# A masked softmax on one core: engines programmed by hand in one critical section, and a mask that skips the left half of the columns behind a branch

## The chip, the cores and the metric

The kernel runs on one core of a Trainium2 chip. The metric is the device time of one execution in microseconds (us). A core has several engines that run their own instruction streams side by side: DVE (the vector engine), ACT (the scalar engine, here for the exponential), POOL, PE (not used for work here) and SP, which in this kernel only issues transfers. Transfers between the large memory (DRAM) and the on-chip memory are done by 16 DMA engines; a transfer of a whole batch is cut over all 16, and each of them works its queue off in order. A semaphore is a counter by which one engine, or a finished transfer, tells another that it may go on.

## The reference

The input `x` has 16 batches, 8 heads and 256 x 256 float32 values for each; each batch has one length. Softmax is taken along the last axis over the first `length` columns, and all columns from there on are zero.

```python
batch, heads, seq_q, seq_k = 16, 8, 256, 256
lengths = np.random.randint(seq_k // 2, seq_k, size=batch)
...
for b in range(batch):
    length = lengths[b]
    masked = x[b, :, :, :length].copy()
    masked = masked - np.max(masked, axis=-1, keepdims=True)
    exp_masked = np.exp(masked)
    result[b, :, :, :length] = exp_masked / np.sum(exp_masked, axis=-1, keepdims=True)
```

The lengths are thus at least 128. The 16 that are drawn, the same in every run, lie between 157 and 252. `x` and the result have 33.55 MB each, and a batch 2 MB each way.

## The kernel before, in words

The 2048 rows of a batch (8 heads x 256) are laid on 128 partitions with 16 rows of 256 columns each, so that one tile `x_tile` holds a whole batch, 128 x 4096 values. There are 12 such buffers (`slots`). All work is done in place in the buffer.

A framework schedules the kernel: it takes the operations in the order of the program text, puts them on their engines, may change the order on an engine by its own estimate, and adds the semaphore waits.

- Line 42, ACT's queue: the 16 lengths are copied to every partition (`len_bcast`, a transfer of 16 KB).
- Line 48, SP: the loads of the batches. The first 12 are issued ahead; load `b + 10` is issued after the store of batch `b`, for `b` from 2 on, into the buffer whose store was issued two batches earlier, and waits for that store. The framework gives the transfers eight semaphores in turn, so that a transfer waits until the one eight places before it has landed.
- Lines 55, 57, 61: POOL writes the column numbers, DVE adds one half and turns the lengths to float.
- Line 67, DVE, once a batch: `cap`, one row of 256 values on every partition, is (column + 0.5 - length) x -1e30. It is a very large positive number in the columns to keep and a very large negative one in the others.
- Line 80, DVE, twice a batch (8 rows per partition each): the minimum of `x_tile` and `cap`, called a clip below. Kept columns stay as they are, and the others become very negative, so that their exponential is zero.
- Line 87, ACT, 16 times a batch: the exponential of one row per partition, with the row's sum as a second result. The maximum is not subtracted.
- Line 93, DVE, twice a batch: the reciprocals of 8 sums. Line 95, DVE, 16 times a batch: each row times its reciprocal.
- Line 102, SP: the store of the batch.

On DVE the scheduler runs about one half batch ahead: a clip of the next half stands between the reciprocals and the multiplications of the last one. SP's queue is in the order of the text: loads 0 to 11, stores 0 to 2, then load 12, store 3, load 13, store 4, load 14, store 5, load 15 and stores 6 to 15.

Of the kernel before, what the change touches and what calls it, by code (L numbers as in the profile page):

```python
# [1 line left out]

# [4 lines left out]


F32 = mybir.dt.float32  # L10
ALU = mybir.AluOpType
EXP = mybir.ActivationFunctionType.Exp


@with_exitstack
def kernel(
    ctx: ExitStack,
    tc: tile.TileContext,
    x: bass.AP,
    lengths: bass.AP,  # L20
    out: bass.AP,
):
    nc = tc.nc
    P = nc.NUM_PARTITIONS

    batch, heads, seq_q, seq_k = x.shape
    rows = heads * seq_q
    assert rows % P == 0
    nt = rows // P

    x_f = x.rearrange("b h q k -> b (h q) k").rearrange("b (p t) k -> b p t k", p=P)
    out_f = out.rearrange("b h q k -> b (h q) k").rearrange("b (p t) k -> b p t k", p=P)

    slots = 12
    ahead = slots - 2

    singles = ctx.enter_context(tc.tile_pool(name="singles", bufs=1))
    work = ctx.enter_context(tc.tile_pool(name="work", bufs=slots))
    small = ctx.enter_context(tc.tile_pool(name="small", bufs=4))

    len_bcast = singles.tile([P, batch], mybir.dt.int64)
    nc.scalar.dma_start(out=len_bcast, in_=lengths.partition_broadcast(P))

    tiles = {}

    def load(b):
        tiles[b] = work.tile([P, nt, seq_k], F32, name="x_tile", tag="x_tile")
        nc.sync.dma_start(out=tiles[b], in_=x_f[b])

    for b in range(min(slots, batch)):  # L50
        load(b)


    iota_i32 = singles.tile([P, seq_k], mybir.dt.int32)
    nc.gpsimd.iota(iota_i32, pattern=[[1, seq_k]], base=0, channel_multiplier=0)  # L55
    iota_h = singles.tile([P, seq_k], F32)
    nc.vector.tensor_scalar(  # L57
        out=iota_h, in0=iota_i32, scalar1=0.5, scalar2=None, op0=ALU.add
    )
    len_f32 = singles.tile([P, batch], F32)  # L60
    nc.vector.tensor_copy(out=len_f32, in_=len_bcast.bitcast(mybir.dt.int32)[:, ::2])  # L61

    for b in range(batch):
        t = tiles.pop(b)

        cap = small.tile([P, seq_k], F32, name="cap", tag="cap")
        nc.vector.tensor_scalar(  # L67
            out=cap,
            in0=iota_h,
            scalar1=len_f32[:, b : b + 1],  # L70
            scalar2=-1.0e30,
            op0=ALU.subtract,
            op1=ALU.mult,
        )
        row_sum = small.tile([P, nt], F32, name="row_sum", tag="row_sum")
        inv_sum = small.tile([P, nt], F32, name="inv_sum", tag="inv_sum")
        half = nt // 2
        for h in range(2):
            s = slice(h * half, (h + 1) * half)
            nc.vector.tensor_tensor(  # L80
                out=t[:, s, :],
                in0=t[:, s, :],
                in1=cap[:, None, :].to_broadcast([P, half, seq_k]),
                op=ALU.min,
            )
            for j in range(h * half, (h + 1) * half):
                nc.scalar.activation(  # L87
                    out=t[:, j, :],
                    in_=t[:, j, :],
                    func=EXP,  # L90
                    accum_out=row_sum[:, j : j + 1],
                )
            nc.vector.reciprocal(out=inv_sum[:, s], in_=row_sum[:, s])  # L93
            for j in range(h * half, (h + 1) * half):
                nc.vector.tensor_scalar(  # L95
                    out=t[:, j, :],
                    in0=t[:, j, :],
                    scalar1=inv_sum[:, j : j + 1],
                    scalar2=None,
                    op0=ALU.mult,  # L100
                )
        nc.sync.dma_start(out=out_f[b], in_=t)
        n = b + ahead
        if b >= 2 and slots <= n < batch:
            load(n)


# [1 line left out]
_INS = ['x', 'lengths']  # L109
_OUTS = [((16, 8, 256, 256), 'float32')]  # L110


# [23 lines left out]
```

## Time and profile before

| | |
|---|---|
| Time, median of 9 runs | 166.24 us (166.08 to 166.58) |
| The profiled execution: its own time | 166.05 us |
| Its span in the profile | 164.3 us |
| DRAM read and written | 33.57 MB and 33.55 MB, 409 GB/s over the span |
| First load and lengths transfer issued | 0.74 and 0.73 us after the start |
| First instruction of DVE on data | 9.83 us, after the lengths have landed |
| Last store issued | 156.0 us |
| From issue to landing, stores | 7.4 us at least, 27.8 in the median, 39.7 at most |
| DVE's instructions | 338 busy ones; 341 in the program |

How to read the profile: the first lines give each engine's busy time, its share of the span and the number of its instructions. Then the span is shown in 40 equal slices of 4.1 us, a digit for each (9 is 90% busy or more); the line DMA is the mean busy share of the 16 DMA engines. The lines on queues give packets, megabytes and the share of the 16 engines' span; q1 is SP's queue, q10 is ACT's, and q14 brings the engines' instructions. The chain that ended last is followed back from the last instruction. A group line has the source line, the engine, the operation, what is written and read with its shape and the number of instructions, then the busy time and the mean of one in nanoseconds, then the idle time just before them. A line of windows gives, for a stretch of time, each engine's busy microseconds and instructions, the clock of PE, the mean share of the DMA engines (packets are counted where they start, so a short window can be over 1) and what they moved. Beside these views the trace has the start and length of each packet and the time of each of the 16 marks by which the DMA engines report their part of a transfer as done.

### The profile page before, as it was taken

To read this page: it belongs to the slowest core of one execution; us is meant where nothing else is said; L and a number is where in the kernel's file an instruction comes from. 1 tells how busy PE (TensorE), PEld (TensorE's weight loads), DVE (VectorE), ACT (ScalarE), POOL (GpSimd) and SP (SyncE) were. 2 spreads that over 40 slices of the span, in tenths; PEclk is the share of its full clock that TensorE was granted. 3 is DMA by queue.
4 is the path that set the end of the run, shared out by engine and by line. 5 is a ranking of instruction groups with operands and counts; after the bars stand their busy time and mean duration, and the time that the engine had idled before them with its cause. 6 is when DMAs were issued, how large, how long until landed. Compare 5 with 4: busy or idle time off the path is not lost.

```text
span 164.3 us, 981 instructions
## 1 busy us (share of the span) xinstructions
DVE 145.0 (88%) x338; ACT 105.9 (64%) x513; POOL 0.5 (0%) x5
## 2 busy tenths in 40 slices
DVE  0059999999999999999999999999999999999700
ACT  0038999177977376938887676937695886947300
POOL 1000000000000000000000000000000000000000
DMA  6999999999999999999999999999999999999793
GB/s 164 334 412 423 443 425 427 421 435 435 423 427 435 423 421 435 435 427 427 423 431 421 431 433 411 439 431 427 427 427 439 431 425 431 433 435 423 339 391 144
DMA packets 4759, 67.18 MB, mean 409 GB/s; under 512 B 656, under 2 KB 656, under 8 KB 656
## 3 DMA queue, kind: packets, MB, share of 16 engines
q1 hardware_dynamic: 4608, 67.11, 96.9%
q14 instruction: 7, 0.06, 0.1%
q10 hardware_dynamic: 144, 0.02, 0.1%
HBM read 33.57 MB, written 33.55 MB: 409 GB/s over the span
## 4 chain that ended last, share of the span: by engine, by line
DVE 86%; DMA 6%; ACT 2%; issue 1%; DVEq 0%; ACTq 0%
DVE x_tile L80 42%; DVE x_tile L95 39%; DMA len_bcast<-in_lengths_dram 6%; DVE inv_sum L93 2%; ACT x_tile L87 2%; DVE cap L67 2%; DVEq L131 0%; DVE iota_h L57 0%; DVE len_f L61 0%; ACTq L131 0%
## 5 line engine op out<-in xcount | busy, mean ns | idle before, releaser
L87 ACT ACTIVATE x_tile<-x_tile 128x256 f32<-128x256 f32 x256 | 102.5, 402 | 37.9 <-issue 23.3
L80 DVE TENSOR_TENSOR x_tile<-x_tile,cap 128x2048 f32<-128x2048 f32 x32 | 72.3, 2261 | 0.0
L95 DVE TENSOR_SCALAR x_tile<-x_tile,inv_sum 128x256 f32<-128x256 f32 x256 | 69.9, 347 | 0.1
L87 ACT ACTIVATION_READ_ACCUMULATOR x_tile<-x_tile 128x1 f32 x256 | 47.9, 187 | 0.0
L61 DVE CAST len_f<-len_bcast 128x16 f32<-128x16 int32 x1 | 0.2, 175 | 9.8 <-DMA len_bcast<-in_lengths_dram 9.8
L87 ACT ACT_TABLE_LOAD x1 | 1.3, 1283 | 9.7 <-DMA x_tile<-in_x_dram 9.7
L93 DVE RECIPROCAL inv_sum<-row_sum 128x8 f32<-128x8 f32 x32 | 6.1, 194 | 1.0 <-ACT x_tile L87 1.0
L67 DVE TENSOR_SCALAR cap<-iota_h,len_f 128x256 f32<-128x256 f32 x16 | 4.8, 316 | 0.0
L55 POOL IOTA iota_i<- 128x256 int32 x1 | 0.3, 342 | 0.4 <-PEq L131 0.4
L57 DVE TENSOR_SCALAR iota_h<-iota_i 128x256 f32<-128x256 int32 x1 | 0.3, 286 | 0.0
L120 POOL MEMSET const-bfloat16-1.0<- 128x1 bf16 x1 | 0.1, 102 | 0.0
L120 POOL MEMSET const-uint8-127<- 128x1 uint8 x1 | 0.1, 102 | 0.0
L120 POOL MEMSET const-float32-0.0<- 128x1 f32 x1 | 0.1, 99 | 0.2 <-issue 0.2
L120 POOL MEMSET const-float32-1.0<- 128x1 f32 x1 | 0.1, 99 | 0.0
## 6 DMA issues: line engine op xcount, KB each, us to landing
x_tile<-in_x_dram SPq DMA_DIRECT2D x16, 2048.0 KB, 25.8
out_dram<-x_tile SPq DMA_DIRECT2D x16, 2048.0 KB, 27.8
len_bcast<-in_lengths_dram ACTq DMA_DIRECT2D x1, 16.0 KB, 9.1
```

The costliest lines, as they stand in the source:

```text
L55: nc.gpsimd.iota(iota_i32, pattern=[[1, seq_k]], base=0, channel_multiplier=0)
L57: nc.vector.tensor_scalar(out=iota_h, in0=iota_i32, scalar1=0.5, scalar2=None, op0=ALU.add)
L61: nc.vector.tensor_copy(out=len_f32, in_=len_bcast.bitcast(mybir.dt.int32)[:, ::2])
L67: nc.vector.tensor_scalar(out=cap, in0=iota_h, scalar1=len_f32[:, b : b + 1], scalar2=-1.0e30, op0=ALU.subtract, op1=ALU.mult,)
L80: nc.vector.tensor_tensor(out=t[:, s, :], in0=t[:, s, :], in1=cap[:, None, :].to_broadcast([P, half, seq_k]), op=ALU.min,)
L87: nc.scalar.activation(out=t[:, j, :], in_=t[:, j, :], func=EXP, accum_out=row_sum[:, j : j + 1],)
L93: nc.vector.reciprocal(out=inv_sum[:, s], in_=row_sum[:, s])
L95: nc.vector.tensor_scalar(out=t[:, j, :], in0=t[:, j, :], scalar1=inv_sum[:, j : j + 1], scalar2=None, op0=ALU.mult,)
L120: nc = _bacc.Bacc("TRN2", target_bir_lowering=False, num_devices=1)
```

## The change

All operations stand in one critical section, in which the framework neither orders nor adds waits: each engine's stream and every semaphore are written out by hand. Entering and leaving the section puts a few control instructions (a no-op, waits, branches) on the engines. Every load and every store has a semaphore of its own (`s_ld`, `s_st`).

- SP issues the same transfers in the same order; the first 12 loads go without any wait, a store waits for `s_out`, loads 12 to 15 wait for the store of the buffer's earlier batch, and at the end SP waits for all stores.
- DVE reads the 16 lengths into registers (two load instructions for 32 words, line 65 of the kernel after).
- The mask of batch `b + 1` is put ahead of the reciprocals and multiplications of batch `b`. It is one clip of the right half of the columns for all 16 rows, 128x16x128, and one of the left half behind a branch that is taken past it when the length is 128 or more (lines 124 and 136 of the kernel after).
- DVE waits for its own reciprocal by a semaphore (`s_v`) before it multiplies. ACT waits once a batch (`s_min`) and reports each half batch (`s_exp`).
- `row_sum` and `inv_sum` have their own place for every batch, and `cap` has four in turn as before.

DVE's program has 377 instructions in place of 341. The core of the diff, with the removed lines left out:

```diff
+    with tc.tile_critical(no_gpsimd_drain=True):
...
+        nc.sync.dma_start(out=xt[0], in_=x_f[0]).then_inc(s_ld[0], 16)
+        nc.scalar.dma_start(out=len_i, in_=lengths.partition_broadcast(P)).then_inc(s_len, 16)
+
+        _, words = nc.values_load_multi_w_load_instructions(
+            lengths.bitcast(I32)[None, :],
+            engines=[DVE],
...
+        lens = words[::2]
...
+        for b in range(1, slots):
+            load(b)
+        for b in range(batch):
+            nc.sync.wait_ge(s_out, b + 1)
+            nc.sync.dma_start(out=out_f[b], in_=xt[b % slots]).then_inc(s_st[b], 16)
+            n = b + slots - behind
+            if b >= behind and n >= slots and n < batch:
+                nc.sync.wait_ge(s_st[n - slots], 16)
+                load(n)
+        for b in range(batch):
+            nc.sync.wait_ge(s_st[b], 16)
...
+        def clip(b, lo, hi):
+            t = xt[b % slots]
+            return nc.vector.tensor_tensor(
+                out=t[:, :, lo:hi],
+                in0=t[:, :, lo:hi],
+                in1=cap[:, b % 4, None, lo:hi].to_broadcast([P, nt, hi - lo]),
                 op=ALU.min,
             )
...
+        def mask(b):
+            if b + 1 < batch and b + 1 not in cap_at:
+                cap_at[b + 1] = make_cap(b + 1)
+            nc.vector.wait_ge(s_v, cap_at[b])
+            nc.vector.wait_ge(s_ld[b], 16)
+            with nc.vector.If(lens[b] < mid):
+                clip(b, 0, mid)
+            clip(b, mid, seq_k).then_inc(s_min, 1)
...
+        mask(0)
+        for b in range(batch):
+            if b + 1 < batch:
+                mask(b + 1)
+            t = xt[b % slots]
+            for h in range(2):
+                s = slice(h * half, (h + 1) * half)
+                nc.vector.wait_ge(s_exp, 2 * b + h + 1)
+                step(nc.vector.reciprocal(out=inv_sum[:, b, s], in_=row_sum[:, b, s]))
+                nc.vector.wait_ge(s_v, v)
+                for j in range(h * half, (h + 1) * half):
+                    ins = nc.vector.tensor_scalar(
...
+            ins.then_inc(s_out, 1)
...
+        for b in range(batch):
+            t = xt[b % slots]
+            nc.scalar.wait_ge(s_min, b + 1)
+            for j in range(nt):
+                ins = nc.scalar.activation(
...
+                if (j + 1) % half == 0:
+                    ins.then_inc(s_exp, 1)
```

## The prediction

> **What bounds the kernel now.** I read the busy lines and the slices of the page first, then the DMA queues, the chain of work that ended last, the groups, and at last the windows of the final microseconds. The page at first accuses DVE:
>
> ```profile
> DVE 145.0 (88%) x338; ACT 105.9 (64%) x513; POOL 0.5 (0%) x5
> ...
> DMA  6999999999999999999999999999999999999793
> ...
> q1 hardware_dynamic: 4608, 67.11, 96.9%
> q14 instruction: 7, 0.06, 0.1%
> ...
> DVE 86%; DMA 6%; ACT 2%; issue 1%; DVEq 0%; ACTq 0%
> ```
>
> The chain gives DVE 86% of the span. But a chain names one path, and the slices show a second resource just as full: the 16 DMA engines stand at 9 tenths from the second slice to the 38th, and SP's queue (q1) holds them for 96.9% of the span. Both resources run from the first microseconds to the last, so which of them sets the end has to be read at the end itself:
>
> ```profile
> core 0: us, DVE busy (x) ACT busy (x) POOL busy (x), PEclk, DMA share, GB/s
> ...
> 10.00:58.00 48.00, 47.96 (x110) 35.57 (x172) 0.00 (x0) 1.00 1.01 429
> 58.00:114.00 56.00, 56.00 (x127) 40.50 (x199) 0.00 (x0) 1.00 1.01 427
> 114.00:153.00 39.00, 38.46 (x94) 29.02 (x143) 0.00 (x0) 1.00 1.01 431
> 153.00:155.00 2.00, 1.45 (x6) 0.48 (x3) 0.00 (x0) 1.00 0.94 401
> 155.00:156.00 1.00, 0.95 (x4) 0.00 (x0) 0.00 (x0) 1.00 0.31 131
> 156.00:157.00 1.00, 0.00 (x0) 0.00 (x0) 0.00 (x0) 1.00 0.69 295
> 157.00:158.00 1.00, 0.00 (x0) 0.00 (x0) 0.00 (x0) 1.00 0.65 279
> 158.00:159.00 1.00, 0.00 (x0) 0.00 (x0) 0.00 (x0) 1.00 1.21 508
> ```
>
> The last two columns are to be read. From 10 to 153 us the DMA engines have no gap (share 1.01) at 427 to 431 GB/s, in loads, mixture and stores alike. The only dip is at 155 to 158 us, when most engines have drained and the last store is issued at 156.0. It is worth 0.69 + 0.31 + 0.35 = 1.35 us of all 16 engines, and it is the only thing in this trace that a faster DVE can fill. I then asked whether it sets the end. The trace keeps 16 completion marks for each transfer, one per DMA engine. For the last but one store they lie at 155.27 to 157.26 us on 14 engines and at 158.21 and 158.56 on the two latest. For the last store 14 lie at 162.06 to 162.24 and two at 163.01 and 163.33. The two late engines took 163.01 - 158.21 = 4.80 and 163.33 - 158.56 = 4.77 us for it, no more than the 4.9 us that every transfer takes on an engine throughout (latest marks of the first four loads: 9.64, 14.51, 19.42, 24.32). So **the two engines that end the kernel never waited for DVE**; the dip is on the other 14. The kernel is bound by the latest DMA engine, and DVE runs just beside it.
>
> **What the change removes.** The drawn lengths are 157 to 252, all at or above 128, so every branch skips the left half. 32 clips of 128x2048 become 16 of 128x16x128, as many elements each:
>
> ```profile
> L80 DVE TENSOR_TENSOR x_tile<-x_tile,cap 128x2048 f32<-128x2048 f32 x32 | 72.3, 2261 | 0.0
> L95 DVE TENSOR_SCALAR x_tile<-x_tile,inv_sum 128x256 f32<-128x256 f32 x256 | 69.9, 347 | 0.1
> L93 DVE RECIPROCAL inv_sum<-row_sum 128x8 f32<-128x8 f32 x32 | 6.1, 194 | 1.0 <-ACT x_tile L87 1.0
> ```
>
> 72.3 / 2 = 36.1 us leave DVE: 145.0 - 36.1 = 108.9 us, with some 0.24 us twice a batch now exposed between reciprocal and first multiplication (150.07 to 150.30 us in the timeline), 16 x 0.48 = 8 us: 117 us, 7.3 a batch against 9.0 (93.92 - 75.92 = 18.0 for two). ACT needs 6.4 a batch (16 x 0.40 from start to start), so DVE stays the slower of the two and is 9.8 + 117 = 127 us in, if nothing stops it. What is late next is the transfer queue, which was never early: 32 x 4.9 = 157 us on each engine. Its order stays as it is, twelve loads, three stores, then load and store in turn, then stores. The last load lands at 114.0 us now, so batch 15 is ready at about 125 and the last store is issued some 30 us sooner. Of the 36 us I therefore book **zero**: the 14 engines close their dip and end earlier, the two late ones do not.
>
> **What it adds on DVE.** All of this has cover. The first store takes its turn behind twelve loads, at 64.1 us (latest mark of load 11), and batch 0 would be ready near 20; the last store has the 30 us above. The 16 compare-and-branch pairs and the two register loads of the lengths are not in this trace. Nearest rows: a DVE semaphore instruction of 21 ns below; above, for the register loads, the 9.1 us landing of the small lengths transfer, each, 18 us at most, which moves batch 0 from 20 to 38, still under 64; for a branch, a whole 8 KB instruction load waited out, 0.31 us in the trace's packets behind one 16 KB packet of 0.61: 2 x 0.92 = 1.8 a batch, with which DVE takes 9.1, its pace of now. None reaches the path by waiting alone. If the cover went, one microsecond a batch would cost 16. DVE also waits for load b+1 before it multiplies batch b; behind that wait stand the reciprocals and multiplications of b, and SP's store of b waits for them. The worst case is batch 14 behind load 15 at 114.0, when its store's turn comes after 150.4 (first mark of store 13): covered by 30 us.
>
> On SP, loads 7 to 11 no longer wait for a free one of eight semaphores, but seven loads were already queued, so nothing starts sooner. SP waits for store b-2 before it loads into that slot, with store b+1 queued behind that wait, exactly as now (43.6 us over four such waits), and two stores are in the rings meanwhile. The lengths transfer leaves from ACT's queue beside the first load as now, so the slow first 9 us (304 GB/s) stay.
>
> **What lies on the path.** Two ends remain. At the start the critical section puts a no-op, a wait of SP on its own semaphore and a branch ahead of the first load; SP's control instructions at the close follow each other at 0.06 us, so 3 x 0.06 = 0.18 us, between 0.06 and 0.4 (the 0.4 being the barrier hop of the first 0.65 us). At the close SP goes through two branches, a no-op that collects five semaphores and another branch, and the other engines wait for it: seven steps of 0.06 less the three trailing waits that go, 0.24 us, between 0 and 0.6. Third, instruction loads share the DMA engines: seven of 8 KB during the run, 0.31 us each in the trace's packets, after which the latest mark of that moment is some 0.45 us later (29.22 to 34.56 is 5.34 us where 4.9 is usual). DVE's program grows from 341 to 377 instructions before its separate waits, so between none and one more such load, on one engine, which need not be the last: 0 to 0.45, I take 0.13.
>
> Sum: 166.05 (profiled execution) + 0.18 + 0.24 + 0.13 = 166.60. That execution lies 0.19 under the median of nine, 166.24, so against the median the sum is 166.79. I forecast **166.7**, between the two.
>
> [...]
>
> **Rivals.**
> 1. *The late engines are late by accident* (faster). Their lag of some 3.3 us was collected in steps from 0.8 us, beside instruction loads and at the turns from loads to stores. If another pace of DVE and ACT spreads these over other engines, the third latest sets the end: 157.26 + 4.85 = 162.1 instead of 163.3, with the two ends 166.24 - 1.2 + 0.4 = 165.4. With all engines even (mean mark 156.07 + 4.85 = 160.9) it would be 164.2. For it: the dip of 1.35 us is real. Against it: the nine runs lie within 0.5 us, so the lag repeats. Chance 0.21, all faster.
> 2. *A jump reloads code* (slower). If each taken branch fetches 8 KB, 16 packets of 0.31 us, 0.45 each with what they push aside, land on the one engine that serves DVE: + 7.2 us, and 166.24 + 0.4 + 7.2 = 173.8. It decides from about one reload a batch. Against it: seven reloads in the whole run now, as many as straight code needs. Chance 0.07.
> 3. *The ends cost more* (slower): both upper bounds and a whole extra load, 0.4 + 0.6 + 0.45 = 1.45, 167.7. Chance 0.10.
> 4. *The skip does not act*, and DVE runs both halves, 32 clips and 145 us. The transfers still bound: 166.7. Chance 0.02.
>
> My forecast, the ends at 166.4 to 167.1, holds the remaining 0.60.
>
> **Chances and range.** A measurement of this kernel can tell some 0.2%, 0.33 us, from no change, so "same" is 165.91 to 166.57. The forecast (with rival 4, 0.62) splits into 0.40 slower, 0.19 same, 0.03 faster; rivals 2 and 3 add 0.17 slower, rival 1 adds 0.21 faster: faster 0.24, same 0.19, slower 0.57. The range reaches into rivals 1 and 3: 165.3 to 168.0.
>
> **What would show it.** Right: DVE near 109 us busy, x16 clips of 2.2 to 2.3 us; DVE idle in the last 30 us; the last stores waiting long in the rings (landing after 30 us or more, where 7.4 is the shortest now); no dip before the last microseconds; the same late end of one or two engines. The q14 row shows the reloads: 7 or 8 bears out the sum, over 20 is rival 2. First load issued at 0.9 instead of 0.74 us shows the start. Wrong: a last mark well before 163 us after the start (rival 1), or DMA share below 0.95 between 10 and 150 us.

## The result, and the profile after

The kernel after takes 167.07 us in the median of 10 runs (166.76 to 167.36); the kernel before, with 30 runs by then, 166.25. The ratio is 1.0048, 95% interval 1.0036 to 1.0060: the change makes the kernel some half per cent slower. The forecast was 166.7, slower. The profiled execution of after is one of its shorter ones, 166.33 us with a span of 164.6, against 166.05 and 164.3 before, so a profile alone shows 0.28 of the 0.82 us.

The page of the kernel after, the same lines as were shown of before:

```profile
DVE 113.9 (69%) x322; ACT 104.9 (64%) x513; POOL 0.5 (0%) x5
...
DMA  2999999999999999999999999999999999999981
...
q1 hardware_dynamic: 4608, 67.11, 96.0%
q14 instruction: 7, 0.06, 0.1%
...
DVE 64%; DVEq 11%; ACT 4%; issue 2%; SPq 0%
```

DVE gave up 145.0 - 113.9 = 31.1 us, and the DMA line is as full as it was. The chain still begins with DVE, at 64%, in a kernel that got slower while DVE got faster: a share of the chain is no price. The groups, in the same order of columns as before:

```profile
L152 DVE TENSOR_SCALAR x<-x,inv_sum 128x256 f32<-128x256 f32 x256 | 70.2, 349 | 1.1
...
L124 DVE TENSOR_TENSOR x<-x,cap 128x2048 f32<-128x2048 f32 x16 | 36.6, 2287 | 0.0
L102 DVE CAST len_f<-len_i 128x16 f32<-128x16 int32 x1 | 0.2, 175 | 17.9 <-issue 17.9
L149 DVE RECIPROCAL inv_sum<-row_sum 128x8 f32<-128x8 f32 x32 | 6.3, 198 | 1.7 <-ACT x L166 1.7
```

16 clips of 2.29 us are left: the skip acts. DVE now starts at 17.9 us. The windows (engines, clock of PE, DMA share, GB/s):

```profile
1.00:10.00 9.00, 0.00 (x0) 1.28 (x1) 0.34 (x1) 1.00 0.74 284
10.00:58.00 48.00, 38.07 (x103) 36.04 (x179) 0.00 (x0) 1.00 1.01 430
58.00:114.00 56.00, 55.44 (x157) 50.83 (x252) 0.00 (x0) 1.00 1.01 429
114.00:153.00 39.00, 20.37 (x65) 16.73 (x84) 0.00 (x0) 1.00 1.01 431
...
157.00:158.00 1.00, 0.00 (x0) 0.00 (x0) 0.00 (x0) 1.00 1.07 459
158.00:159.00 1.00, 0.00 (x0) 0.00 (x0) 0.00 (x0) 1.00 0.99 426
159.00:160.00 1.00, 0.00 (x0) 0.00 (x0) 0.00 (x0) 1.00 0.73 311
160.00:161.00 1.00, 0.00 (x0) 0.00 (x0) 0.00 (x0) 1.00 0.31 131
161.00:162.00 1.00, 0.00 (x0) 0.00 (x0) 0.00 (x0) 1.00 0.27 115
162.00:163.00 1.00, 0.00 (x0) 0.00 (x0) 0.00 (x0) 1.00 0.04 16
```

The dip at 155 to 158 us is gone, the rate between 10 and 153 us is the same, and the end is a slope: from 159 us on fewer and fewer DMA engines have anything left. The completion marks of the last store say it by engine: 12 of them at 160.07 to 161.23 us, the last four at 162.26, 162.77, 162.93 and 163.24. Before, the last mark was at 163.33.

The stores now wait in the queue and not for DVE: the last one is issued at 134.6 us and lands 28.6 us later, and none lands sooner than 19.0 us after its issue, where 7.4 was the least before.

```profile
L80 SPq DMA_DIRECT2D out_dram<-x x16: 332/338/695, 30.2 to 134.6; - x16
...
DMA to landing us min/median/max: 19.0/33.5/39.8
```

### The profile page after: what moved, and what is told of

It is laid out like the page before. It is cut to its first block, busy times and chain, and to the rows that moved or that the text cites. A ratio compares the mean times of both kernels' runs of the same rounds, so it can differ in the third digit from the quotient of the medians.

```text
span 164.6 us, 968 instructions
## 1 busy us (share of the span) xinstructions
DVE 113.9 (69%) x322; ACT 104.9 (64%) x513; POOL 0.5 (0%) x5
## 4 chain that ended last, share of the span: by engine, by line
DVE 64%; DVEq 11%; ACT 4%; issue 2%; SPq 0%
DVE x L152 39%; DVE x L124 20%; DVEq L65 10%; ACT x L166 4%; DVE inv_sum L149 2%; DVE cap L109 2%; DVEq L136 0%; DVE iota_h L104 0%; DVE len_f L102 0%; DVEq L199 0%; SPq L50 0%
## 5 line engine op out<-in xcount | busy, mean ns | idle before, releaser
L166 ACT ACTIVATE x<-x 128x256 f32<-128x256 f32 x256 | 102.3, 402 | 25.5 <-DVE x L124 25.5
L152 DVE TENSOR_SCALAR x<-x,inv_sum 128x256 f32<-128x256 f32 x256 | 70.2, 349 | 1.1
L166 ACT ACTIVATION_READ_ACCUMULATOR x<-x 128x1 f32 x256 | 48.0, 187 | 0.0
L124 DVE TENSOR_TENSOR x<-x,cap 128x2048 f32<-128x2048 f32 x16 | 36.6, 2287 | 0.0
L102 DVE CAST len_f<-len_i 128x16 f32<-128x16 int32 x1 | 0.2, 175 | 17.9 <-issue 17.9
L109 DVE TENSOR_SCALAR cap<-iota_h,len_f 128x256 f32<-128x256 f32 x16 | 5.5, 349 | 0.0
```

What stands on the lines that cost most here:

```text
L102: step(nc.vector.tensor_copy(out=len_f, in_=len32[:, ::2]))
L109: nc.vector.tensor_scalar(out=cap[:, b % 4, :], in0=iota_h, scalar1=len_f[:, b : b + 1], scalar2=-1.0e30, op0=ALU.subtract, op1=ALU.mult,)
L124: return nc.vector.tensor_tensor(out=t[:, :, lo:hi], in0=t[:, :, lo:hi], in1=cap[:, b % 4, None, lo:hi].to_broadcast([P, nt, hi - lo]), op ...
L152: ins = nc.vector.tensor_scalar(out=t[:, j, :], in0=t[:, j, :], scalar1=inv_sum[:, b, j : j + 1], scalar2=None, op0=ALU.mult,)
L166: ins = nc.scalar.activation(out=t[:, j, :], in_=t[:, j, :], func=EXP, accum_out=row_sum[:, b, j : j + 1],)
```

## The experiments

All times are medians; every ratio is to the kernel before, run beside it on the same chip.

**One part alone: the right half in the framework (run tile_right).**

```diff
 nc.vector.tensor_tensor(
-    out=t[:, s, :],
-    in0=t[:, s, :],
-    in1=cap[:, None, :].to_broadcast([P, half, seq_k]),
+    out=t[:, s, seq_k // 2 :],
+    in0=t[:, s, seq_k // 2 :],
+    in1=cap[:, None, seq_k // 2 :].to_broadcast([P, half, seq_k // 2]),
     op=ALU.min,
 )
```

> The kernel before with one part of the change alone: its two clips a batch take only the right 128 columns (the left half is left out without any branch; with these lengths it changes nothing). DVE loses some 36 us of work. Theory (the latest DMA engine ends the kernel and never waits for DVE): no gain, 166.25 us, between 165.9 and 166.6; the dip in the DMA share at 155 to 158 us goes. Rival 1 (the dip counts, the freed DVE time shortens the end): 164.9 us. Rival 2 (DVE is the bound, as the chain of waits says): about 135 to 140 us of DVE work and then the transfers, again 164 to 165 us, with the last store issued long before.

Measured: 166.36 us, ratio 0.9997 (0.9988 to 1.0007). DVE is busy for 112.7 us, the last store is issued at 136.6 in place of 156.0, and nothing is gained. The last marks (14 engines at 160.0 to 161.1, two at 163.58 and 163.75) show why: the 14 end earlier, the two do not. Both rivals fall.

**The section without register loads and branch (run crit_right).**

```diff
-        _, words = nc.values_load_multi_w_load_instructions(...)
...
-            with nc.vector.If(lens[b] < mid):
-                clip(b, 0, mid)
             clip(b, mid, seq_k).then_inc(s_min, 1)
```

> The kernel after without the register loads and without the branch: the right half is clipped, the left half is left out. DVE starts at some 9 us in place of 17.9. Theory (register loads and branches are covered, the loss lies in the two ends of the critical section): as the kernel after, 167.0 us, between 166.7 and 167.4. Rival (the branch, or the 15 us register load, costs the time): 166.3 us or less.

Measured: 166.89 us, ratio 1.0037 (1.0024 to 1.0050), which overlaps that of the kernel after. So registers and branches cost 0.2 us, if anything. The same half mask in the framework, on the same chip, took 166.36 us: the section with its hand-written streams costs 0.53 us even without registers and branches. The 0.2 us are little for what the register loads do to DVE in the kernel after (rows of its sequencer: number, ns at least, in the median and at most, first and last start):

```profile
L65 DVEq TENSOR_LOAD <-in_lengths_dram_ptr x1: 1783/1783/1783, 1.0 to 1.0; - x1
L65 DVEq TENSOR_LOAD <-in_lengths_dram x1: 15041/15041/15041, 2.8 to 2.8; - x1
```

The two loads hold DVE for 16.8 us; a delay of 8 us at DVE's start goes under, as the first store's turn comes at 64 us. A branch takes 56 ns, and there are as many instruction loads, seven, as before.

**The section with the whole mask: where the cover ends (run crit_full).**

```diff
-            with nc.vector.If(lens[b] < mid):
-                clip(b, 0, mid)
-            clip(b, mid, seq_k).then_inc(s_min, 1)
+            clip(b, 0, seq_k).then_inc(s_min, 1)
```

(The register loads go too.)

> The kernel after with the mask of before: one clip of all 256 columns a batch, no register load, no branch. Each batch costs DVE 2.2 us more, so 7.2 + 2.2 = 9.4 us a batch, 9.5 + 16 x 9.4 = 160 us, and the last store is issued at 160 and lands at 167.5. Theory (DVE is covered only as long as it issues the last store before its turn at some 155 to 158 us): 170.5 us, between 169 and 172. Rival (DVE work does not matter in this section at all): 167.0 us.

Measured: 168.62 us, ratio 1.0130 (1.0112 to 1.0147). The sign is the theory's, the size is 1.9 us under it and just below its range: a batch takes DVE 9.28 us, not 9.4, the last store is issued at 159.0, not 160, and its last mark comes 6.5 us later, not 7.5: at 165.49, 4.9 us after that of the store before it. The windows show the hole that a late DVE makes in the transfers, which no run with the half mask has:

```profile
142.00:146.00 4.00, 3.96 (x14) 4.00 (x21) 0.00 (x0) 1.00 0.88 377
146.00:150.00 4.00, 3.96 (x3) 1.48 (x8) 0.00 (x0) 1.00 1.06 449
150.00:154.00 4.00, 3.96 (x17) 4.00 (x22) 0.00 (x0) 1.00 0.25 107
154.00:158.00 4.00, 3.93 (x17) 2.13 (x12) 0.00 (x0) 1.00 0.78 328
158.00:162.00 4.00, 0.95 (x4) 0.00 (x0) 0.00 (x0) 1.00 1.03 434
```

So the half mask is worth 168.62 - 166.89 = 1.7 us inside the section, where a batch of the whole mask takes DVE 9.28 us in place of 9.0, and nothing in the framework.

**The transfers alone, in the framework (run tile_copy) and in the section (run crit_copy).** Every operation on DVE, ACT and POOL is taken out; loads and stores keep their order, and a store waits for its load.

> The transfers of the kernel before alone: the same loads and stores in the same order, with the lengths transfer, and no work on DVE, ACT or POOL (the output is x itself; all of the softmax is left out). Theory (the latest DMA engine sets the end): the time stays within 1.5 us of the kernel before, 165.0 to 166.3 us, best value 165.5; what is missing are the instruction loads of DVE and ACT, which the late engines collect. Rival (work on DVE or ACT sets the end): 163 us or less.

Measured: 164.03 us (163.23 to 164.71), ratio 0.9864 (0.9836 to 0.9892). This is 1.0 us below the theory's range and 1.0 above the rival's, and decides for neither as worded. All but 2.3 of the 166.34 us of the kernel before are those of the bare transfers, and what makes the 2.3 was still to be shown.

> The transfers of the kernel after alone, in the critical section, with no work on the other engines (the output is x itself; all of the softmax is left out), no register load and no branch. Theory (the loss lies in entering and leaving the section): slower than the transfers in the framework by the same 0.6 to 0.8 us as the kernel after against the kernel before. Rival (the loss comes from the programs on DVE and ACT): the same as the transfers in the framework, within 0.2 us.

Measured: 166.34 us, ratio 0.9977 (0.9954 to 1.0000), 2.3 us over the transfers in the framework, with a wide spread (164.63 to 166.57). The section is dearer without any program on DVE or ACT, which goes against the rival; but 2.3 is three times the theory's 0.6 to 0.8. Of the profiled pair 0.5 us lie at the close (1.21 us from the last mark to the end, against 0.72) and 1.45 at the last mark (162.84 against 161.39). With no instruction load at all, the latest engine of the section's transfers ends 2.40 us behind the first (160.44); its latest mark makes steps of 5.16, 5.52 and 5.47 us at the transfers that end at 78.7, 103.8 and 114.2, while loads and stores alternate. In the framework, too, three steps there are longer than the usual 4.9: 5.20, 5.20 and 5.15.

**Programs beside the transfers (run copy_instr).** To the transfers alone, 256 exponentials and 339 multiplications on scratch rows are added, which nothing waits for:

```diff
...
+    for i in range(256):
+        nc.scalar.activation(out=scr_a, in_=scr, func=EXP, accum_out=sums[:, i : i + 1])
...
+    for i in range(339):
+        nc.vector.tensor_scalar(out=scr_v, in0=scr, scalar1=0.5, scalar2=None, op0=ALU.mult)
```

> The transfers alone, as in the run tile_copy, and beside them DVE and ACT work through programs as long as those of the kernel before (339 multiplications and 256 exponentials) on scratch rows that no transfer touches (all of the softmax is left out). Theory (8 KB instruction loads share the DMA engines, and the engines that serve them end late): some 7 instruction loads in the run in place of none, and the time back from 164.0 to 165.5 to 166.4 us, best value 166.0. Rival (it is the work on the batch buffers themselves that slows the transfers): 164.0 us as without programs.

Measured: 165.79 us, ratio 0.9967 (0.9956 to 0.9978): 1.76 of the 2.3 us between the bare transfers and the kernel before come back with programs that touch no batch buffer. First the queues of the bare transfers, then those with programs:

```profile
q1 hardware_dynamic: 4608, 67.11, 97.9%
q10 hardware_dynamic: 144, 0.02, 0.1%
HBM read 33.57 MB, written 33.55 MB: 414 GB/s over the span
```

```profile
q1 hardware_dynamic: 4608, 67.11, 96.8%
q14 instruction: 7, 0.06, 0.1%
q10 hardware_dynamic: 144, 0.02, 0.1%
HBM read 33.57 MB, written 33.55 MB: 409 GB/s over the span
```

The row q14 is the one that is new. It is 0.1% of the DMA engines' time, yet the last engine lies 1.6 us behind the first at the end of the bare transfers (161.39 and 159.84) and 3.5 behind with programs (163.27 and 159.80). The run adds the instruction loads and the work on the scratch rows together; no run has one without the other.

**Fewer instructions on DVE (run tile_mul1).** The clip of tile_right, and a half batch multiplied at once:

```diff
...
-            for j in range(h * half, (h + 1) * half):
-                nc.vector.tensor_scalar(
...
+            nc.vector.tensor_tensor(
+                out=t[:, s, :],
+                in0=t[:, s, :],
+                in1=inv_sum[:, s, None].to_broadcast([P, half, seq_k]),
+                op=ALU.mult,
+            )
```

> The kernel before with the right half alone clipped (as tile_right) and with one multiplication of 128x2048 in place of eight of 128x256, so that DVE's program falls from 341 to some 115 instructions at the same DVE time. Theory (instruction loads make the late engine late): 2 or 3 of the 7 instruction loads go, 0.45 us each if they fall on the latest engine, 165.3 us, between 164.8 and 166.0. Rival (the number of instructions does not matter while DVE is covered): 166.35 us as tile_right.

Measured: 166.24 us, ratio 0.9992 (0.9982 to 1.0003). The theory missed: the loads fell from 7 to 5 and the time did not move.

```profile
q14 instruction: 5, 0.04, 0.1%
```

Either the loads do not matter, against the run before, or only those that fall on one engine do.

**ACT's program alone (run copy_act).** The run with programs, less the multiplications on DVE.

> The transfers with ACT's program of 256 exponentials on scratch rows alone; DVE's 339 multiplications are left out against copy_instr, and all of the softmax is. Theory (fewer DVE instructions did nothing in tile_mul1, so the DMA engine that ends last is the one that serves ACT's instruction loads): 4 loads, and 165.3 to 165.9 us, as copy_instr. Rival (every instruction load counts alike): 4 of the 7 loads, 164.03 + 4/7 x 1.76 = 165.0 us. Rival (DVE's loads are those that count): 164.0 to 164.4 us, as without programs.

Measured: 165.49 us, ratio 0.9953 (0.9940 to 0.9967), which is 165.2 to 165.7 at the 166.22 of the kernel before beside it; both rivals lie outside.

```profile
q1 hardware_dynamic: 4608, 67.11, 96.7%
q10 hardware_dynamic: 144, 0.02, 0.1%
q14 instruction: 4, 0.03, 0.0%
```

The four loads of ACT's program do nearly all that seven did. In the trace they start at 17.3, 51.9, 87.1 and 121.9 us, and the latest mark, which advances by 4.9 us a transfer, advances by 5.54, 5.47 and 5.42 at the transfers that end at 54.1, 88.6 and 124.6. In tile_mul1 the loads at ACT's pace (22.7, 50.9, 79.6 and 114.2) are all still there, and the latest mark makes steps of 5.58 at 54.5, 5.52 at 84.3 and 6.09 at 115.4.

That the DMA engine that serves ACT's loads is the one that ends last can be followed in the packets of copy_act. The trace does not name the engines, but 2931 of the 4103 packets of 8 or 16 KB in before, and 3029 in after, start exactly 4 ns before another one ends. Taken as the step from one packet to the next on the same engine, this lets packets be strung together. All four loads then stand in one string, and it is the one that ends last. The loads and the packets that they stretch (to 0.86, 0.86, 0.72 and 0.72 us from 0.61) take 1.9 us on it, as much as the last mark moved from the bare transfers (163.31 against 161.39).

They are not all of the lag. The same string has packets of 1.37 and 1.38 us at 91.2 and 101.0 us with no load beside them (steps of 5.47 at 94.1 and 5.58 at 104.5), and tile_mul1 has such a step, 5.53 at 94.7. In the kernel after the latest mark makes only two long steps, 5.50 at 104.6 with no load beside it and 5.38 at 119.6 behind two loads (115.2 and 117.9). That ACT's loads set the end there is not shown.

**The small packets of the lengths (runs tile_len_sp, tile_len_pe and crit_len_pe).** First the same transfer from SP's queue, ahead of the first load:

```diff
-    nc.scalar.dma_start(out=len_bcast, in_=lengths.partition_broadcast(P))
+    nc.sync.dma_start(out=len_bcast, in_=lengths.partition_broadcast(P))
```

> The kernel before with one edit: the lengths transfer leaves from SP's queue ahead of the first load, not from ACT's queue beside it. The question is what the slow first 9 us (304 GB/s) cost on the path. Theory (small packets of a second queue alternate with the large ones and stretch them from 0.61 to some 0.78 us, nine times on each DMA engine, and the latest engine carries that to the end): 1.0 to 1.5 us faster, 165.0 us. Rival (the slow start is the cost of the first large reads themselves): 166.6 us, slower by the 0.4 us that the extra issue takes.

Measured: 166.19 us, ratio 0.9991 (0.9981 to 1.0001): neither number. DVE started at 4.3 us, but the first load was issued at 1.17 us and not 0.74, and the latest mark of load 1 is 14.62 against 14.51: what the first loads gained by it, the later issue took. Inconclusive for the question. Then one row, spread by PE:

```diff
-    nc.scalar.dma_start(out=len_bcast, in_=lengths.partition_broadcast(P))
...
+    nc.scalar.dma_start(out=len_row, in_=lengths[None, :])
...
+    nc.tensor.matmul(len_ps, lhsT=ones, rhs=len_row_f, start=True, stop=True)
...
```

> The kernel before with the lengths fetched in one row, a single packet on one DMA engine, and spread to the partitions by PE (a product with a row of ones) in place of 128 packets of 128 bytes. Theory (the small packets stretch the first nine large ones on every engine): 1.5 us faster, between 1.0 and 2.5, 164.8 us, and DVE starts at 4 to 6 us. Rival (the slow start is the cost of the first large reads): 166.3 us, no change.

Measured: 165.53 us, ratio 0.9948 (0.9936 to 0.9960). The packets do cost time on the path, 0.8 us, half of what was expected. Window 1 to 10 us of the kernel before, and below it of this run, in which the columns PE and its weight loads stand ahead of DVE:

```profile
1.00:10.00 9.00, 0.17 (x2) 0.29 (x1) 0.17 (x1) 1.00 0.90 304
```

```profile
1.00:10.00 9.00, 0.60 (x2) 0.50 (x2) 2.62 (x6) 1.28 (x1) 0.17 (x1) 1.00 0.93 353
```

353 GB/s in place of 304. The same edit in the kernel after, with its own wait and product on PE:

> The kernel after with one edit: the lengths come in one row and are spread by PE, so that no small packets alternate with the first loads. Theory (the section costs 0.2 us at the start and 0.38 at the close; what else the kernel after lost, one DMA engine 1.6 us later after the second load, is the small packets, which now come ahead of the first load): 165.5 + 0.6 = 166.1 us, between 165.8 and 166.4. Rival (the small packets have no part in it): 166.9 to 167.1 us as the kernel after, less the 0.8 us that the same edit gave the kernel before at most.

Measured: 166.02 us, ratio 0.9983 (0.9973 to 0.9993), the theory's number. The rival is not ruled out: 0.8 us off its 166.9 is 166.1. The edit takes 1.05 us from the kernel after and 0.81 from the kernel before, and with intervals of some 0.2 us to either side of each ratio the two gains cannot be told apart.

**Both gains together (run tile_both).**

> The run tile_mul1 together with the lengths spread by PE (as tile_len_pe): the version that should beat both kernels. Theory: both gains add, 165.3 - 0.8 = 164.5 us, between 164.0 and 165.2. Rival (both shorten the same lag and only one counts): 165.3 us.

Measured: 165.63 us, ratio 0.9954 (0.9939 to 0.9970), no better than the lengths by PE alone, as tile_mul1 had gained nothing. The fastest version found with the whole computation is the kernel before with the lengths spread by PE, 165.53 us, which beats both kernels.

## Why the prediction was right, point by point

- *The latest DMA engine ends the kernel and never waited for DVE; the 36 us count zero.* Shown, by tile_right (DVE 32.3 us lighter, ratio 0.9997) and by crit_full, which has the price when the cover does go.
- *DVE's busy time.* 108.9 expected, 113.9 measured: 31.1 us went and not 36.1. The rows of DVE's groups add to 153.6 us before, where DVE is busy for 145.0, as instructions overlap at their ends (a clip ends at 145.84 us, and the multiplication behind it starts at 145.76); a clip that goes freed 31.1 / 16 = 1.94 us, less than its own 2.26. A batch takes 7.14 us (clips start 30.44 and 37.58), 7.3 were expected; the last store was issued at 134.6 and not at 125, because DVE began at 17.9 and then never waited for a load.
- *Register loads between 21 ns and 18 us, branches below 0.92, all covered.* 16.8 us and 56 ns, and crit_right puts their price at some 0.2 us, within the intervals. The trace shows seven instruction loads before, without these branches, and seven after, where each of the 16 is taken, so a reload at each of them (rival 2) did not come about. The second of the two register loads takes 15.04 us for 32 words, 0.47 us each, beside full transfer queues.
- *The start, 0.18 us.* The first load is issued at 0.94 in place of 0.74, 0.21 us. *The close, 0.24 us.* From the last mark to the end it is 164.55 - 163.24 = 1.31 us against 164.26 - 163.33 = 0.93, so 0.38. *Between none and one more instruction load, 0.13.* None: 7 and 7. The three terms measure 0.59 against 0.55. That the start reaches the end is not shown: in the profiled pair the last mark comes 0.09 us earlier than before, so their 0.28 us are the 0.38 of the close less that. What the section costs as a whole is shown by two pairs of runs: 166.89 - 166.36 = 0.53 us with the same half mask (crit_right and tile_right), and 166.02 - 165.53 = 0.49 with the lengths spread by PE. The sum had the size of the section right; how it divides is argued from one trace of each kernel.
- *"The lengths transfer leaves from ACT's queue beside the first load as now, so the slow first 9 us (304 GB/s) stay."* This step is wrong. ACT issues the lengths at 0.90 us and SP, behind its no-op, the first load at 0.94, where both were issued at 0.73 and 0.74 before. In this execution the small packets come first: they start at 1.92 in place of 2.77 us, the first large one at 2.56 in place of 1.76, and window 1 to 10 falls from 304 to 284 GB/s. The latest mark of load 1 goes from 14.51 to 16.13 us, and it is 16.05 in crit_right; in crit_full, where SP was 30 ns behind ACT and not 40, the large packets were first (1.97 against 3.11 us) and the mark is 14.73. The order alone does not make the 1.6 us: in crit_copy the small packets are first too (1.92 against 2.42 us), and the mark is 14.85.
- *The 0.27 us by which the measured 0.82 passes the sum's 0.55.* This stays open. The wrong step above may be part of it: the kernel after gains 0.24 us more than the kernel before when the small packets go. But that is within the intervals, and in the profiled execution the last mark is no later for them.
- *Rival 1, that the lag of the late engines is an accident which another pace spreads.* It did not come about: with another pace of DVE the latest mark was 163.75 us (tile_right) and 163.24 (after), against 163.33. Why the lag repeats is known in part. ACT's instruction loads come at two paces, every 35 us in copy_act and every 28 to 35 us in tile_mul1, and add to it in copy_act; but crit_copy ends with a lag of 2.40 us without any load, and gathers most of it while loads and stores alternate.

Open stays why the bare transfers in the section take 2.3 us more than in the framework, where the start and the close above make 0.59; and why their times fall into two clusters, five at 164.6 to 165.8 and seven at 166.3 to 166.6 us. The profile caught one of the former.

## What to carry to other kernels

When the slices show two resources full, as here (DVE busy for 88% of the span, SP's queue 96.9%), neither the busy share nor the chain (86% DVE) says which one sets the end: look at the last transfer's completion marks engine by engine, and ask of the latest one alone whether it ever waited. Work taken off an engine that is covered was worth nothing here (32.3 us of DVE in tile_right, ratio 0.9997), so weigh an edit first by what it adds at the two ends and on the queues of the DMA engines. This kernel, bound by its transfers, was made faster by taking away 128 packets of 128 bytes that shared the DMA engines with them (0.8 us), and not by two instruction loads less (tile_mul1, ratio 0.9992).

## What the runs showed of the hardware that was not expected

- Programs of some 850 instructions beside the transfers cost them 1.8 us (165.79 against 164.03), though the seven instruction loads of 8 KB are 0.1% of the DMA engines' time. With ACT's program alone (165.49) its four loads all fall on the engine that ends last, and they and the packets behind them take 1.9 us there.
- The engine that runs the instructions does not show its four instruction loads in copy_act: ACT's instructions start 0.22 or 0.32 us apart from the first to the last. The transfers beside them pay some 0.5 us a load on the latest DMA engine at three of the four (steps of 5.42 to 5.54 us in place of 4.9).
- In the kernel after SP's issue of a load took 5.0, 4.2 and 4.2 us for the tenth, eleventh and twelfth that it issued without waits, where the first nine took 0.4 to 1.2 us each; an estimate from these twelve is that the queue takes some nine transfers of 2 MB ahead. The DMA share stayed at 1.01 from 10 us on, and nothing was lost by it.
- SP's first load was issued 6 and 30 ns behind ACT's small transfer in before and crit_full, where the large packets moved first, and 34 to 40 ns behind it in crit_copy, crit_right and after, where the small ones did. With the small ones first, one DMA engine was 1.3 to 1.6 us later at the second load in two of these three (16.05 and 16.13 against 14.51 and 14.73), and not in crit_copy (14.85).
